# Four edits at the end of a hybrid encoder layer: last stores on ScalarE's queue, a weight sum on GpSimd, low parts regrouped, two row halves finished in PSUM banks

## Chip, core and metric

The kernel runs on one core of a Trainium2 chip. The metric is the device time of one execution in microseconds (us). The engines are called by the profile's names: PE is TensorE (PEld its weight loads), DVE is VectorE, ACT is ScalarE, POOL is GpSimd and SP is SyncE, which in the kernel before issues nearly all DMA transfers.

## The reference

One encoder layer over 1024 tokens and 1024 channels, in float32. What matters here is its end:

```
y_a = attn * silu(z_a);  y_b = h * silu(z_b)
m   = sigmoid(g_a + b0) * (y_a @ w_ba) + sigmoid(g_b + b1) * (y_b @ w_bb)
out = layer_norm(ALPHA * x + m @ w_out, ln_g, ln_b)
```

`y_a` is the attention branch with 512 channels and `y_b` the recurrent one. `x` is the layer's input after an embedding LayerNorm. The last LayerNorm runs over the 1024 channels of each token.

## The kernel before

**Number format.** Every product keeps float32 accuracy with three matmuls on reduced operands: a value is split into a high part (a cast, made on ACT by `high`, line 1317) and a low part (the value minus its high part, made by `lo_of`, line 128, on DVE or POOL), and high times high, low times high and high times low are summed in PSUM (`mm3`, line 134).

**Branch's projection.** The last part of the kernel is a list of numbered slots. In slots 0 to 15 PE multiplies `y_a` by `w_ba`: slot 2j+n is output channel block j (128 channels) and token half n (512 tokens), 12 matmuls each. In the next slot DVE gates the result with g_a (line 1021) and adds the other branch's part (`merge`, line 1331); the sum is a 128x512 block of `m`. The blocks are at once split and combined for the next product.

**Output product.** `m @ w_out` is computed as a 2x2 block product in Strassen-Winograd form: seven products instead of eight. The four blocks of `m` give a11, a12, a22 and the sums s1 to s4; the four blocks of `w_out` give b11, b21, b22 and the sums t1 to t4. Each operand is four tiles of 128x512, c = 0 to 3 (the contraction). `t1(c) = b12 - b11`, `t2(c) = b22 - t1`, `t3(c) = b22 - b12` (written over b12) and `t4(c) = b21 - t2` (written over b21). Slots 16 on walk over PLAN and LAST: a11 times b11 for the four row blocks p = 0 to 3, then a12 with b21, s2 with t2, s1 with t1 for p = 0, 1, s4 with b22 for p = 0, 1, then both for p = 2, 3, then s3 with t3 and a22 with t4. The PSUM bank `banksX[p]` collects a11, s2, s3 and a22, `banksW[p]` a12, s1 and s4. The very last product (a22 with t4, p = 3) is made in two column halves into banks y.

**Evacuation.** After a product, DVE adds the bank to the residual tile `zs[p, r, n]` (128 tokens by 512 channels; r is upper or lower row half of the grid, n the channel half; loaded by `z_load`, line 1413): `begun` (line 1500) or `added` (line 1503), then `seen` (line 1466) takes the row statistics. When both halves of a row are there, `finished(p, r)` runs: `mean_var` (line 1485), `newton` (a square root on ACT at line 1471, a refinement of four small DVE steps, lines 1472 to 1478), the bias on DVE (line 1491), then for each n one ACT pass over z (line 1494), two POOL passes with the gain and the offset (lines 1495 and 1496) and one store from SP (line 1497). This is done for seven of the eight rows. The eighth (p = 3, r = 1) is finished on DVE in quarters (lines 1586 to 1600) with four stores from SP (line 1601).

**What sets the order.** Every engine runs its instructions in the order in which the code is written. `job(slot, f)` puts a function on a slot's list, and the list runs in the order of entry before the slot's product is issued. An instruction that waits holds everything behind it on its engine, and a store that waits holds SP's later transfers. `w_low` (on POOL) reuses, for each new low part, the tile that the `w_low` before it has freed.

Of the kernel before, what the change touches and what calls it, by code (L numbers as in the profile page):

```python
# [25 lines left out]
EPS = 1e-5  # L26
TWICE = 4.0
# [40 lines left out]
def encoder_kernel(ctx, tc, x, gb1, gb, w_qk, w_v, w_s, w_ba, w_bb, w_gate, smalls, bias, w_out, out):  # L68
    nc = tc.nc
    V, A, G, PE, SP = nc.vector, nc.scalar, nc.gpsimd, nc.tensor, nc.sync  # L70

    def pool(name, side="left", **kw):
        return tc.alloc_tile_pool(name=name, bufs=1, side=side, reuse_waits="tile", **kw)
# [131 lines left out]
    halves = [slice(c * HALF, (c + 1) * HALF) for c in range(2)]  # L205
# [83 lines left out]
    def f(t, i):  # L289
        return t[:, :, ti(i)].bitcast(F32)  # L290
# [751 lines left out]
    for slot in range(7 * N_PAIR + 4):  # L1042
        p, k = divmod(slot, 7)
# [184 lines left out]
    for unit in range(-NT, H * NT + PV_LAG):  # L1228
        h, c = divmod(unit, NT)
# [49 lines left out]
        if unit == H * NT:  # L1279
# [3 lines left out]
            wop = pool("wop", "right")  # L1283
            raw = {}
# [18 lines left out]
    def job(slot, f, *args):  # L1303
        jobs.setdefault(slot, []).append(lambda: f(*args))
# [10 lines left out]
    def high(o, c, src, pl, tag, **kw):  # L1315
        t = hi[o, c] = place((o, "h", c), pl, tag, **kw)
        A.copy(t[:], src)

    def low(o, c, src, pl, tag, eng=V):
        t = lo[o, c] = place((o, "l", c), pl, tag)  # L1320
        lo_of(eng, t[:], src, hi[o, c][:])

    def minus(out_, a, b, eng=V):
        eng.tensor_tensor(out_, a, b, ALU.subtract)
# [50 lines left out]
    for slot in range(16):  # L1375
        j, n = divmod(slot, 2)
# [15 lines left out]

    def t3(c):
        t = raw["t3", c] = raw["b12", c]
        minus(t[:], raw["b22", c][:], t[:])

    def t4(c):
        t = raw["t4", c] = raw["b21", c]
# [2 lines left out]
    def w_high(o, c, pl, tag, **kw):  # L1401
        high(o, c, raw[o, c][:], pl, tag, **kw)
# [3 lines left out]
    def w_low(o, c, full, *home):  # L1406
        homes[o, c] = spare.pop()
        spare.append(home)
        low(o, c, full[:], *homes[o, c], G)

    def z_load(p, r, n, pl, tag, **kw):
        z = zs[p, r, n] = pl.tile([P, HALF], F32, tag=tag, name=f"z{p}{r}{n}", **kw)
        SP.dma_start(z[:], h_d[p + 4 * r][:, halves[n]])
# [5 lines left out]
    zs, gbs = {}, {}  # L1419
    for c in range(4):  # L1420
        if c > 1:
            job(c - 2, w_load, "b12", c)
            job(c - 2, w_load, "b11", c)
        job(c + 4, w_load, "b22", c)
        job(c + 6, w_load, "b21", c)
        job(2 * c + 3, t1, c)
        job(2 * c + 4, lambda c: w_high("b11", c, wop, f"b11h{c}"), c)
        job(2 * c + 5, lambda c: w_low("b11", c, raw["b11", c], wop, f"b11{c}"), c)
        job(c + 10, lambda c: w_high("b21", c, *((ap, f"b21h{c}") if c < 3 else (wop, "b21h3"))), c)
        job(16, lambda c: low("b21", c, raw["b21", c][:], yap, f"y1{c}1", G), c)  # L1430
        job(16 + c, lambda c: z_load(c, 0, 0, ev, "z", bufs=5), c)
        job(17, gb_load, c // 2, c % 2)
        job(17, t2, c)
        job(18 + c, t4, c)
        job(17 + c, lambda c: w_high("t2", c, yap, f"y1{c}0"), c)
        job(18 + c, lambda c: w_low("t2", c, raw["t2", c], yap, f"y0{c}1"), c)
        job(18 + c, lambda c: high("s1", c, late["m", c, 1][:], yap, f"y0{c}0"), c)
        job(19 + c, lambda c: w_high("t1", c, ev, *((f"u{c + 1}",) if c < 3 else ("z",)), **({} if c < 3 else dict(bufs=5))), c)
        job(20 + c, lambda c: w_low("s1", c, late["m", c, 1], late["mp"], f"m{c}1"), c)
        job(24 + c, t3, c)  # L1440
        job(21 + c, lambda c: z_load(c, 0, 1, ap, f"a11l{c}"), c)
        job(22 + c, lambda c: w_high("b22", c, wop, f"b11h{c}"), c)
        job(22 + c, lambda c: w_low("t1", c, raw["t1", c], wop, f"t1{c}"), c)
        job(24 + c, lambda c: w_low("b22", c, raw["b22", c], wop, f"b22{c}"), c)
        job(25 + c, lambda c: w_high("t3", c, ap, f"a11h{c}"), c)
        job(25 + c, lambda c: z_load(c, 1, 1, ap, f"a12h{c}"), c)
        job(28 + c, lambda c: w_low("t3", c, raw["t3", c], wop, f"b12{c}"), c)
        job(25 + c, lambda c: high("s3", c, raw["s3", c][:], ap, f"s3h{c}"), c)
        job(27 + c, lambda c: low("s3", c, raw["s3", c][:], *((ap, f"s3l{c - 1}") if c else (wop, "spare3"))), c)
        job(26 + c, lambda c: w_high("t4", c, *homes["b11", c]), c)  # L1450
        job(30 + c, lambda c: w_low("t4", c, raw["t4", c], wop, f"b21{c}"), c)
        job(29 + c, lambda c: z_load(c, 1, 0, ap, f"a12l{c}"), c)

    zp, banksX, banksW, stats = None, {}, {}, {}

    def small(name, n, tag, bufs):
        return zp.tile([P, n], F32, tag=tag, bufs=bufs, name=name)
# [7 lines left out]
            c += n * len(pieces)  # L1465
            V.bn_stats(st[:, 6 * c:6 * c + 6], src[:, part])

    def newton(mv, name, other):

        sd, ve = small(f"sd{name}", 1, "sd", 2), small(f"ve{name}", 3, "ve", 2)  # L1470
        A.activation(sd[:], mv[:, 1:2], AF.Sqrt, bias=eps_z[:])
        V.tensor_scalar(ve[:, 0:1], mv[:, 1:2], EPS * TWICE * TWICE, -0.5, ALU.add, ALU.mult)
        next(other, None)
        V.reciprocal(sd[:], sd[:])
        next(other, None)
        V.tensor_scalar(ve[:, 1:2], sd[:], sd[:], ve[:, 0:1], ALU.mult, ALU.mult)
        next(other, None)
        V.tensor_scalar(sd[:], ve[:, 1:2], 1.5, sd[:], ALU.add, ALU.mult)
        for _ in other:
            pass  # L1480
        return sd, ve

    def mean_var(p, r):
        mv = small(f"mv{p}{r}", 2, "mv", 2)
        V.bn_aggr(mv[:], stats[p, r][:].rearrange("p (c s) -> p c s", s=6))
        return mv

    def finished(p, r):
        mv = mean_var(p, r)
        sd, ve = newton(mv, f"{p}{r}", iter(()))  # L1490
        V.tensor_scalar(ve[:, 2:3], mv[:, 0:1], -1.0, sd[:], ALU.mult, ALU.mult)
        for n in range(2):
            z = zs[p, r, n]
            A.activation(z[:], z[:], AF.Identity, bias=ve[:, 2:3], scale=sd[:])
            G.tensor_tensor(z[:], z[:], gbs[0, n][:], ALU.mult)  # L1495
            G.tensor_tensor(z[:], z[:], gbs[1, n][:], ALU.add)  # L1496
            SP.dma_start(out[p + 4 * r][:, halves[n]], z[:])

    def begun(z, o):
        V.scalar_tensor_tensor(z[:], z[:], ALPHA * TWICE, o[:], ALU.mult, ALU.add)  # L1500
# [46 lines left out]
    for slot in range(16 + len(plan)):  # L1547
        j, n = divmod(slot, 2)
        if slot == 2:
            at0.release()  # L1550
            ap = pool("ap")
            split(0)
        if slot == 3:
            split(1)
        if slot == 16:
            zp = pool("zp")
        if slot < 16 and n == 0 and j > 0:
            b_split(0, j + 1, A)
        for f in jobs.pop(slot, ()):
            f()  # L1560
        if slot < 16:
            if n == 0:
                b_load(0, j + 2)
            g_load(0, j + 1, n, **(dict(tag=f"u{slot % 4}", bufs=1) if slot % 4 else dict(tag="z", bufs=5)))
            o = got[slot] = ring(slot, f"mb{j}{n}")
            run(b_group(0, j, n, ya, o, range(3 if slot < 2 else 4)))
            if 0 < slot < 3:
                run(b_group(0, 0, slot - 1, ya, got[slot - 1], range(3, 4)))
            if 0 < slot < 3:
                merge(slot - 1)  # L1570
            continue
        a, b, p = plan[slot - 16]
        if a == "a11":
            banksX[p] = ring(slot, f"x{p}")
        elif a == "a12":
            banksW[p] = ring(slot, f"w{p}")
        if slot < 16 + len(plan) - 1:
            o = banksX[p] if a in ("a11", "s2", "s3", "a22") else banksW[p]
            o_product(a, b, p, o[:], first=a in ("a11", "a12", "s1"), last=a in ("a12", "s4", "a22"))
    assert not jobs, sorted(jobs)  # L1580

    p, x, w = 3, banksX[3], banksW[3]
    for c, part in enumerate((slice(0, 256), slice(256, HALF))):
        o = ring(c, f"y{c}")
# [4 lines left out]
    mv = mean_var(p, 1)  # L1589

    def scaled():
        for n, part in pieces:
            o = (w, x)[n][:, part]
            V.scalar_tensor_tensor(o, o, mv[:, 0:1], gbs[0, n][:, part], ALU.subtract, ALU.mult)
            yield

    sd, ve = newton(mv, "last", scaled())
    for n, part in pieces:
        z = zs[p, 1, n]
        V.scalar_tensor_tensor(z[:, part], (w, x)[n][:, part], sd[:], gbs[1, n][:, part], ALU.mult, ALU.add)  # L1600
        SP.dma_start(out[p + 4][:, halves[n]][:, part], z[:, part])
# [86 lines left out]
```

## Time and profile before

| what | value |
|---|---|
| median of 3 runs | 673.86 us (673.41 to 674.18) |
| the profiled execution | 674.84 us, of which the span is 673.0 us |
| PE busy | 652.1 us (97%) |
| DVE, ACT, POOL busy | 529.2, 384.6, 403.6 us |
| slots 0 to 15 (branch's projection) | 535.7 to 579.3 us |
| slots 16 on, to PE's last matmul | 579.3 to 657.9 us |
| from PE's last matmul to the end | 15.1 us |

The span is the time between the first and the last recorded event; 1.84 us of the execution's time lie around it. Timeline rows give an instruction's start and duration in us from the span's start, its engine and line, the tiles that it writes and reads, and in brackets how long its engine was idle before it and who ended that. A row with x2 merges two neighbours, and its duration then covers both.

### The profile page before, as it was taken

The numbers are of one execution on the slowest core, as the hardware profiler recorded it, in microseconds if no ns is written. First come the engines' busy times: TensorE is split into PE (matmuls) and PEld (weight loads), VectorE is DVE, ScalarE is ACT, GpSimd is POOL, SyncE is SP. The second block draws the span as 40 slices with busy tenths as digits, with TensorE's granted clock in tenths as the row PEclk, the third lists the DMA queues.
The fourth block names the chain that finished last, engine by engine and source line by source line (L and its number), as shares of the span: only waits on it lengthen the run. The fifth ranks groups of instructions, "written<-read, shape, count | busy, mean of one in ns | idle before, by whom it ended". The sixth has DMA issues, their size and how long they took to land.

```text
span 673.0 us, 9451 instructions
## 1 busy us (share of the span) xinstructions
PE 652.1 (97%) x3129; PEld 543.1 (81%) x3129; DVE 529.2 (79%) x872; ACT 384.6 (57%) x662; POOL 403.6 (60%) x315
## 2 busy tenths in 40 slices
PE   8999999999999999999999999999999999998990
PEld 6888888888888887888788888888888888887880
DVE  6978866986998699879968785377777777996674
ACT  5555433357786676669576634477777645463331
POOL 4898263434676576567647535115264468699996
PEclk9999999999999999999999999999999999999996
DMA  8646616133334123431453547998784496340123
GB/s 325 240 157 220 211 39 216 51 117 118 126 131 137 45 96 125 173 126 47 174 196 105 191 158 261 346 330 306 258 314 165 141 318 215 125 150 7 62 99 121
DMA packets 52337, 113.42 MB, mean 169 GB/s; under 512 B 5488, under 2 KB 10176, under 8 KB 50752
## 3 DMA queue, kind: packets, MB, share of 16 engines
q1 hardware_dynamic: 52256, 112.81, 48.7%
q8 instruction: 25, 0.41, 0.2%
q14 instruction: 24, 0.20, 0.1%
q10 hardware_dynamic: 32, 0.01, 0.0%
HBM read 77.11 MB, written 35.68 MB: 168 GB/s over the span
## 4 chain that ended last, share of the span: by engine, by line
PE 67%; DVE 9%; POOL 9%; issue 4%; ACT 1%; DMA 1%; SPq 0%; POOLq 0%; DVEq 0%; ACTq 0%
PE a L134 28%; PE mb L134 13%; PE s L134 11%; PE acc L1147 4%; PE s L1101 3%; PE x L134 3%; PE pt L1123 3%; POOL z L1495 3%; POOL z L1496 2%; PE g L794 2%; PE w L134 2%; POOL ht_l L128 1%; DVE ws_l L128 1%; DVE wa_l L128 1%; POOL t3l L128 1%
## 5 line engine op out<-in xcount | busy, mean ns | idle before, releaser
L134 PE MATMUL a<-ht_h,ws_h 128*128 128x512 f32 x136 | 53.1, 391 | 0.0
L134 PE MATMUL a<-ht_h,ws_l 128*128 128x512 f32 x136 | 53.0, 389 | 0.0
L134 PE MATMUL a<-b_h,wa_l 128*128 128x512 f32 x136 | 53.0, 389 | 0.0
L134 PE MATMUL a<-b_h,wa_h 128*128 128x512 f32 x136 | 52.9, 389 | 0.0
L134 PE MATMUL a<-ht_l,ws_h 128*128 128x512 f32 x136 | 52.9, 389 | 0.0
L134 PE MATMUL a<-b_l,wa_h 128*128 128x512 f32 x136 | 52.9, 389 | 0.0
L1111 DVE CUSTOM_DVE_ANT_0 sc<-s,bias 128x384 f32<-128x384 f32 (+1 forms) x64 | 33.5, 523 | 21.5 <-PE s L1101 14.1
L1131 ACT CAST pt_h<-pt 128x384 fp32r<-128x384 f32 x64 | 29.0, 453 | 25.3 <-PE pt L1123 17.3
L1116 ACT ACTIVATE p<-sc,summ 128x384 f32<-128x384 f32 (+1 forms) x64 | 37.8, 591 | 5.3 <-DVE summ L1111 5.0
L134 PE MATMUL mb<-ya,wb_h 128*128 128x512 f32 x128 | 39.6, 389 | 0.0
L902 POOL CAST wb_h<-wb 128x512 fp32r<-128x512 f32 x9 | 7.0, 780 | 47.5 <-DMA wb<-in_w_bb_dram 47.5
L128 DVE TENSOR_TENSOR pt_l<-pt,pt_h 128x384 fp32r<-128x384 f32 x64 | 33.3, 520 | 2.1 <-ACT pt_h L1131 1.6
L128 POOL TENSOR_TENSOR ht_l<-t,ht_h 128x512 fp32r<-128x512 f32 x16 | 22.0, 1409 | 19.9 <-ACT ht_h L312 19.9
L326 PE MATMUL v<-wv,b_h 128*128 128x512 f32 x128 | 33.1, 399 | 0.6 <-ACT b_h L279 0.5
L1101 PE MATMUL s<-ks,qs 128*128 128x384 f32 (+1 forms) x128 | 31.4, 326 | 0.0
L134 PEld LDWEIGHTS a<-ht_h,ws_h 128*128 128x128 f32 x136 | 25.5, 188 | 6.0 <-issue 0.4
L1123 PEld LDWEIGHTS pt<-ident,p 128*128 128x128 f32 x176 | 23.1, 140 | 8.5
L134 PEld LDWEIGHTS a<-b_h,wa_h 128*128 128x128 f32 x136 | 25.5, 188 | 5.4
L134 PEld LDWEIGHTS a<-ht_l,ws_h 128*128 128x128 f32 x136 | 25.5, 188 | 5.4
L134 PEld LDWEIGHTS a<-b_l,wa_h 128*128 128x128 f32 x136 | 25.5, 188 | 5.3
L134 PEld LDWEIGHTS a<-b_h,wa_l 128*128 128x128 f32 x136 | 25.5, 188 | 5.3
L134 PEld LDWEIGHTS a<-ht_h,ws_l 128*128 128x128 f32 x136 | 25.5, 188 | 5.2
(541 smaller groups left out, 2270.5 us busy)
## 6 DMA issues: line engine op xcount, KB each, us to landing
ks<-k_d SPq DMA_DIRECT2D x8, 1024.0 KB, 7.4
h_d<-x SPq DMA_DIRECT2D x8, 512.0 KB, 4.4
v_d<-vs SPq DMA_DIRECT2D x8, 512.0 KB, 3.5
q_d<-q SPq DMA_DIRECT2D x8, 512.0 KB, 3.0
ga_d<-ga SPq DMA_DIRECT2D x16, 256.0 KB, 2.2
gb_d<-gb SPq DMA_DIRECT2D x16, 256.0 KB, 2.5
k_d<-k SPq DMA_DIRECT2D x8, 512.0 KB, 3.3
qs<-q_d SPq DMA_DIRECT2D x8, 512.0 KB, 5.5
```

The lines of the kernel that those rows point to most:

```text
L128: eng.tensor_tensor(lo, full, hi.bitcast(F32), ALU.subtract)
L134: PE.matmul(o, a, b, start=first and i == 0, stop=last and i == len(prods) - 1, skip_group_check=not (first and last))
L326: PE.matmul(vos[i][:], a, wv[kind == "w"][k][:], start=vn[i] == 0, stop=vn[i] == 23)
L794: PE.matmul(o[:, n, :], w[:, 2 * d + b, :], us[b][:, n * HALF:(n + 1) * HALF], start=z == 0, stop=z == 1)
L1101: PE.matmul(o[:, :P * len(near(t))], q[:, t * P:(t + 1) * P], k[:, z, keys], start=z == 0, stop=z == 1)
L1111: V.tensor_tensor_reduce(s[:, :w], o[:, :w], heads[h][2][:, b0:b0 + w], -1.0, 3.0e38, ALU.add, ALU.min, accum_out=sums[h][0][:, t:t + 1])
L1116: A.activation(probs[h % 2][t][:], scs.pop((h, t))[:, :w], AF.Exp, bias=sums[h][0][:, t:t + 1], scale=-1.0, accum_out=sums[h][1][:, t:t + 1])
L1123: PE.transpose(tp[:, n * P:(n + 1) * P], probs[h % 2][t][:, z * P:(z + 1) * P], ident[:])
L1131: A.copy(pt[0][:, span(b)], tps[h, b][:, :P * len(near(b))])
L1147: PE.matmul(acc[g][:, d:d + w], vvs[h // 2][:, b, h % 2, :], pt[:, a:a + w], start=b in (1, 6) and z == 0, stop=z == 1 and b == (4, 7)[g])
L1495: G.tensor_tensor(z[:], z[:], gbs[0, n][:], ALU.mult)
L1496: G.tensor_tensor(z[:], z[:], gbs[1, n][:], ALU.add)
```

## The change

Four edits.

1. The four last stores (p = 3, r = 1) are issued on ACT's queue, not on SP's.
2. `t3` is computed on POOL, not on DVE, and in slots 10 to 13, inside the branch's projection, not in slots 24 to 27.
3. POOL's low parts are reordered: the low parts of b22 move from slots 24 to 27 to slots 26 to 29, so that those of t1 come ahead of them; those of t3 and then of t4 all stand in slot 30, ahead of every `finished`. The loads of the z tiles (p, 1, 0) move from slots 29 to 32 to slots 25 to 28.
4. `finished`: the two small steps on the mean and the variance (lines 1472 and 1491 before) go from DVE to three small ACT steps. For the rows (0, 0) and (1, 0), half n = 1, ACT writes its pass into `banksW[p]` in PSUM, and DVE does the gain and the offset there in slots 33 and 34, in place of POOL.

```
     def t3(c):
         t = raw["t3", c] = raw["b12", c]
-        minus(t[:], raw["b22", c][:], t[:])
+        minus(t[:], raw["b22", c][:], t[:], G)
...
-        job(24 + c, t3, c)
+        job(10 + c, t3, c)
...
-        job(24 + c, lambda c: w_low("b22", c, raw["b22", c], wop, f"b22{c}"), c)
+        job(26 + c, lambda c: w_low("b22", c, raw["b22", c], wop, f"b22{c}"), c)
...
-        job(28 + c, lambda c: w_low("t3", c, raw["t3", c], wop, f"b12{c}"), c)
...
-        job(30 + c, lambda c: w_low("t4", c, raw["t4", c], wop, f"b21{c}"), c)
-        job(29 + c, lambda c: z_load(c, 1, 0, ap, f"a12l{c}"), c)
+        job(25 + c, lambda c: z_load(c, 1, 0, ap, f"a12l{c}"), c)
+    for o, home in (("t3", "b12"), ("t4", "b21")):
+        for c in range(4):
+            job(30, lambda o, home, c: w_low(o, c, raw[o, c], wop, f"{home}{c}"), o, home, c)
...
         A.activation(sd[:], mv[:, 1:2], AF.Sqrt, bias=eps_z[:])
-        V.tensor_scalar(ve[:, 0:1], mv[:, 1:2], EPS * TWICE * TWICE, -0.5, ALU.add, ALU.mult)
+        if eng is A:
+            A.activation(ve[:, 0:1], mv[:, 1:2], AF.Identity, bias=eps_h[:], scale=-0.5)
+            A.activation(ve[:, 2:3], mv[:, 0:1], AF.Copy, scale=-1.0)
+        else:
+            V.tensor_scalar(ve[:, 0:1], mv[:, 1:2], EPS * TWICE * TWICE, -0.5, ALU.add, ALU.mult)
...
-        sd, ve = newton(mv, f"{p}{r}", iter(()))
-        V.tensor_scalar(ve[:, 2:3], mv[:, 0:1], -1.0, sd[:], ALU.mult, ALU.mult)
+        sd, ve = newton(mv, f"{p}{r}", iter(()), A)
+        A.activation(ve[:, 1:2], ve[:, 2:3], AF.Copy, scale=sd[:])
         for n in range(2):
             z = zs[p, r, n]
-            A.activation(z[:], z[:], AF.Identity, bias=ve[:, 2:3], scale=sd[:])
+            mine = n == 1 and (p, r) in IN_BANK
+            A.activation((banksW[p] if mine else z)[:], z[:], AF.Identity, bias=ve[:, 1:2], scale=sd[:])
+            if mine:
+                continue
...
+    IN_BANK = ((0, 0), (1, 0))
+
+    def finished_in_bank(p, r):
+        w, z = banksW[p], zs[p, r, 1]
+        V.tensor_tensor(w[:], w[:], gbs[0, 1][:], ALU.mult)
+        V.tensor_tensor(z[:], w[:], gbs[1, 1][:], ALU.add)
+        SP.dma_start(out[p + 4 * r][:, halves[1]], z[:])
+
+    for p, r in IN_BANK:
+        job(33 + p, finished_in_bank, p, r)
...
-        SP.dma_start(out[p + 4][:, halves[n]][:, part], z[:, part])
+        A.dma_start(out[p + 4][:, halves[n]][:, part], z[:, part])
```

**POOL in slots 10 to 16.** Before, POOL's order around the last blocks of the branch's projection is this (wb_l is the low part of a projection weight, a12l that of a block of `m`, b11l and b21l those of `w_out`):

```order
L128 TENSOR_TENSOR a12l_5883<-m_4834,a12h_5849 128x512
L128 TENSOR_TENSOR b11l_5919<-wb_3_5622,b11h_5887 128x512
L128 TENSOR_TENSOR wb_l<-wb_5889,wb_h 128x512
L128 TENSOR_TENSOR a12l_5949<-m_5058,a12h_5908 128x512
L128 TENSOR_TENSOR a12l_6007<-m_5260,a12h_5970 128x512
L128 TENSOR_TENSOR a12l_6060<-m_5468,a12h_6024 128x512
L128 TENSOR_TENSOR b21l_6062<-wb_0_5765,b21h_5885 128x512
```

After, on POOL at the same place (the rows of L1324 are the four t3):

```order
L128 TENSOR_TENSOR a12l_5883<-m_4834,a12h_5849 128x512
L1324 TENSOR_TENSOR wb_0_5572<-wb_0_5708,wb_0_5572 128x512
L1324 TENSOR_TENSOR wb_1_5576<-wb_1_5738,wb_1_5576 128x512
L128 TENSOR_TENSOR b11l_5921<-wb_3_5622,b11h_5888 128x512
L128 TENSOR_TENSOR wb_l<-wb_5890,wb_h 128x512
L128 TENSOR_TENSOR a12l_5951<-m_5058,a12h_5909 128x512
L1324 TENSOR_TENSOR wb_2_5602<-wb_2_5769,wb_2_5602 128x512
L1324 TENSOR_TENSOR wb_3_5620<-wb_3_5801,wb_3_5620 128x512
L128 TENSOR_TENSOR a12l_6011<-m_5260,a12h_5973 128x512
L1577 MEMSET eps_h 128x1
L128 TENSOR_TENSOR a12l_6066<-m_5468,a12h_6028 128x512
L128 TENSOR_TENSOR b21l_6068<-wb_0_5765,b21h_5885 128x512
```

Two t3 stand ahead of the last b11l and the last wb_l, and two ahead of the third a12l.

**POOL's low parts.** Before, from the third low part of t1 on, POOL runs these (z are the passes of `finished`, gb the gain or the offset):

```order
L128 TENSOR_TENSOR b22l_6288<-wb_0_5708,b22h_6237 128x512
L128 TENSOR_TENSOR t1l_6292<-t_5799,t1h_6214 128x512
L128 TENSOR_TENSOR b22l_6316<-wb_1_5738,b22h_6263 128x512
L128 TENSOR_TENSOR t1l_6320<-t_5858,t1h_6245 128x512
L128 TENSOR_TENSOR b22l_6344<-wb_2_5769,b22h_6290 128x512
L128 TENSOR_TENSOR b22l_6370<-wb_3_5801,b22h_6318 128x512
L128 TENSOR_TENSOR t3l_6385<-wb_0_5572,t3h_6309 128x512
L128 TENSOR_TENSOR t3l_6412<-wb_1_5576,t3h_6337 128x512
L128 TENSOR_TENSOR t4l_6431<-wb_0_5765,t4h_6335 128x512
L128 TENSOR_TENSOR t3l_6435<-wb_2_5602,t3h_6363 128x512
L1495 TENSOR_TENSOR z_6064<-z_6064,gb_6094 128x512
```

After, on POOL from the same place on:

```order
L128 TENSOR_TENSOR t1l_6295<-t_5799,t1h_6220 128x512
L128 TENSOR_TENSOR t1l_6322<-t_5858,t1h_6251 128x512
L128 TENSOR_TENSOR b22l_6337<-wb_0_5708,b22h_6243 128x512
L128 TENSOR_TENSOR b22l_6364<-wb_1_5738,b22h_6269 128x512
L128 TENSOR_TENSOR b22l_6391<-wb_2_5769,b22h_6293 128x512
L128 TENSOR_TENSOR b22l_6418<-wb_3_5801,b22h_6320 128x512
L128 TENSOR_TENSOR t3l_6437<-wb_0_5572,t3h_6312 128x512
L128 TENSOR_TENSOR t3l_6439<-wb_1_5576,t3h_6341 128x512
```

Every t1l now stands ahead of every b22l. Behind these rows come the two other t3l, the four t4l and then the first pass over z; before, that pass stood behind the third t3l.

**The end of ACT's queue.** After, ACT's order from the last `finished` (p = 2, r = 1) on is this (rows of DMA are transfers that ACT issues; sd, ve and mv are columns of one number per row; before, no DMA stood here):

```order
L1472 ACTIVATE sd_6755<-mv_6753,eps_z 128x1
L1474 ACTIVATE ve_6756<-mv_6753,eps_h 128x1
L1475 ACTIVATE ve_6756<-mv_6753 128x1
L1496 ACTIVATE ve_6756<-ve_6756,sd_6755 128x1
L1500 ACTIVATE z_6374<-z_6374,ve_6756,sd_6755 128x512
L1500 ACTIVATE z_6370<-z_6370,ve_6756,sd_6755 128x512
L1472 ACTIVATE sdlast<-mv_6802,eps_z 128x1
L1622 DMA out_dram<-z_6401 128x256 x2
L1622 DMA out_dram<-z_6397 128x256 x2
```

The four stores are the last rows of ACT, behind nothing that waits for POOL, and each `finished` has three small rows more on ACT.

More of the change, by code (lines that the diff above doesn't have):

```diff
@@ L1466, in seen, with newton @@
             V.bn_stats(st[:, 6 * c:6 * c + 6], src[:, part])
-    def newton(mv, name, other):
+    def newton(mv, name, other, eng=V):
         sd, ve = small(f"sd{name}", 1, "sd", 2), small(f"ve{name}", 3, "ve", 2)
         A.activation(sd[:], mv[:, 1:2], AF.Sqrt, bias=eps_z[:])
-        V.tensor_scalar(ve[:, 0:1], mv[:, 1:2], EPS * TWICE * TWICE, -0.5, ALU.add, ALU.mult)
+        if eng is A:
[3 more added lines that the diff above has]
+            V.tensor_scalar(ve[:, 0:1], mv[:, 1:2], EPS * TWICE * TWICE, -0.5, ALU.add, ALU.mult)
         next(other, None)
@@ L1556, in encoder_kernel @@
             zp = pool("zp")
+            eps_h = zp.tile([P, 1], F32, name="eps_h")
+            G.memset(eps_h[:], -0.5 * EPS * TWICE * TWICE)
         if slot < 16 and n == 0 and j > 0:
```

## Prediction

> **What bounds the kernel now.** I read the page's chain of work first, then the last rows of each engine, then the waits of SP.
>
> ```profile
> span 673.0 us, 9451 instructions
> PE 67%; DVE 9%; POOL 9%; issue 4%; ACT 1%; DMA 1%; SPq 0%; POOLq 0%; DVEq 0%; ACTq 0%
> ```
>
> PE carries the chain for most of the span, but POOL has 9%, some 60 us. The last rows of each engine show where that share lies:
>
> ```profile
> 657.58 0.28 PE L134 MATMUL y<-t4l,a22h 128*128 128x256 f32 x1
> 660.54 0.29 ACT L1471 ACTIVATE sdlast<-mv,eps_z 128x1 f32<-128x1 f32 x1 [0.58 <-DVE mv L1485]
> 663.36 0.87 DVE L1600 SCALAR_TENSOR_TENSOR z<-x,sdlast,gb 128x256 f32<-128x256 f32 x2
> 664.23 1.26 POOL L1496 TENSOR_TENSOR z<-z,gb 128x512 f32<-128x512 f32 x1
> 665.45 1.26 POOL L1495 TENSOR_TENSOR z<-z,gb 128x512 f32<-128x512 f32 x1
> 666.79 1.26 POOL L1496 TENSOR_TENSOR z<-z,gb 128x512 f32<-128x512 f32 x1
> 668.50 1.86 SPq L1601 DMA_DIRECT2D out_dram<-z  x4
> ```
>
> PE ends at 657.9, ACT at 660.8, DVE at 664.2, POOL at 668.05, and SP issues until 670.4. The four last stores have their data when DVE ends, but the first is issued 4.3 us later, because SP holds them behind a store that waits for POOL:
>
> ```profile
> SPq L1497 <- POOL z L1496: 59.1, 14, 26.4
> L1497 SPq DMA_DIRECT2D out_dram<-z x14: 332/332/338, 629.0 to 668.1; - x14
> L1601 SPq DMA_DIRECT2D out_dram<-z x4: 383/397/408, 668.5 to 670.0; - x4
> DMA to landing us min/median/max: 1.9/2.0/2.2
> ```
>
> The end is thus the last issue (670.0), some 2.1 until it has landed and 0.9 more to the end of the span. Ahead of it POOL is the bound, because it hardly idles in the whole output product:
>
> ```profile
> 582.00:604.00 22.00, 22.00 (x98) 18.14 (x97) 21.07 (x30) 10.78 (x21) 21.53 (x16) 1.00 0.42 135
> 630.00:668.00 38.00, 27.85 (x135) 23.36 (x133) 25.29 (x68) 9.38 (x16) 36.83 (x30) 0.90 0.28 103
> ```
>
> In these two windows (length, then busy time of PE, PEld, DVE, ACT and POOL) POOL is busy 21.5 of 22 and 36.8 of 38 us.
>
> **Stores on ACT's queue.** After its last square root ACT holds nothing that could delay the four stores. This alone takes the end from the last issue of the four (670.0) to POOL's own last store (668.1): **-1.9 us**.
>
> **Two row halves in banks.** They take four of POOL's 28 passes away:
>
> ```profile
> L1495 POOL TENSOR_TENSOR z<-z,gb 128x512 f32<-128x512 f32 x14 | 18.0, 1286 | 1.1 <-ACT z L1494 1.1
> 630.54 0.69 DVE L1500 SCALAR_TENSOR_TENSOR z<-z,w 128x512 f32<-128x512 f32 x1 [1.66 <-PE w L134]
> 633.26 0.69 DVE L1503 TENSOR_TENSOR z<-z,w 128x512 f32<-128x512 f32 x1 [2.03 <-PE w L134]
> ```
>
> A pass starts 1.22 or 1.34 after the one before it (rows above), so four are some 5.2, and POOL would end at 662.8 if its data were there. DVE gets four passes more in slots 33 and 34, at the 0.69 of these rows 2.8 us, and it idles there 1.66 + 2.03 us for PE. I cost them at nothing; without this cover DVE is late by up to 2.8.
>
> The data are not there, however. The last row that POOL finishes gets its ACT pass late:
>
> ```profile
> 657.06 0.29 ACT L1471 ACTIVATE sd<-mv,eps_z 128x1 f32<-128x1 f32 x1 [2.81 <-DVE ve L1472]
> 658.14 0.21 DVE L1491 TENSOR_SCALAR ve<-mv,sd 128x1 f32<-128x1 f32 x1
> 658.45 1.52 ACT L1494 ACTIVATE z<-z,ve,sd 128x512 f32<-128x512 f32 x2 [1.10 <-DVE ve L1491]
> ```
>
> Its first half is ready at 658.45 + 0.76 = 659.2, and four passes of 5.2 to 5.3 us in all end at 664.5. With an empty backlog POOL ends there: 664.5 - 668.05 = **-3.55 us**. From then on POOL follows PE and DVE one for one.
>
> **Small steps on ACT.** Each `finished` loses two DVE steps (one beside the square root, and the 0.21 of L1491 in the path) and gains three on ACT of the kind of the 0.29 row. Two of them run while DVE takes the reciprocal; the third stands where the 0.21 stood. The bounds are -0.2 (all hidden) and +0.7 (all in series); I take **+0.1**, from 0.29 against 0.21.
>
> **Low parts regrouped.** PE stands still once in the output product:
>
> ```profile
> 614.23 0.39 PE L134 MATMUL w<-t1h,s1l 128*128 128x512 f32 x1
> 616.39 0.50 PE L134 MATMUL w<-t1l,s1h 128*128 128x512 f32 x1 [1.77 <-POOL t1l L128]
> 614.74 1.59 POOL L128 TENSOR_TENSOR t1l<-t,t1h 128x512 fp32r<-128x512 f32 x1
> 619.46 0.39 PE L134 MATMUL w<-b22h,s4h 128*128 128x512 f32 x1
> 636.36 1.52 ACT L1494 ACTIVATE z<-z,ve,sd 128x512 f32<-128x512 f32 x2 [1.04 <-DVE ve L1491]
> ```
>
> From 616.39 to 619.46 are 13 matmuls, 0.236 each; at 614.23 the next came after 2.16: 1.9 lost. With t1l ahead of b22l, two POOL operations of about 1.6 leave the queue of the last t1l, which then ends at 613.1, while PE asks at 614.5: the stall goes, **-1.9 us**. Late next is b22l: four at 1.4 from 613.1 end at 618.7, and PE asks for the last 11 matmuls after 619.46 - 1.9, at 620.1. The eight low parts of t3 and t4 then end near 630, and the first two rows' passes near 635. The third row's data (636.36, first half 0.76 later, less what PE gains) come after that, so POOL idles ahead of it and follows PE from there. The z loads come earlier and nothing waits for them: nothing.
>
> **t3 on POOL in the projection.** DVE is spared t3 in a stretch where it idles for PE between them, so the removal gives nothing by itself:
>
> ```profile
> L1324 DVE TENSOR_TENSOR wb<-wb,wb 128x512 f32<-128x512 f32 x4 | 5.6, 1396 | 0.0
> 570.98 1.30 POOL L128 TENSOR_TENSOR wb_l<-wb,wb_h 128x512 fp32r<-128x512 f32 x1 [2.48 <-ACT wb_h L900]
> 574.29 1.29 POOL L128 TENSOR_TENSOR a12l<-m,a12h 128x512 fp32r<-128x512 f32 x1 [0.76 <-ACT m L1339]
> 581.18 1.29 POOL L128 TENSOR_TENSOR a12l<-m,a12h 128x512 fp32r<-128x512 f32 x1 [5.60 <-ACT m L1339]
> ```
>
> POOL has room: it idles 2.48, 0.76 and 5.60 us there, and four t3 at 1.25 to 1.3 take 5.2. The catch is DVE, which works beside POOL there and without a gap:
>
> ```profile
> 567.18 1.32 POOL L128 TENSOR_TENSOR b11l<-wb,b11h 128x512 fp32r<-128x512 f32 x1
> 568.54 0.70 DVE L1324 TENSOR_TENSOR mb<-m,m 128x512 f32<-128x512 f32 x1
> L1324 DVE TENSOR_TENSOR mb<-m,m x4: 699/1220/1575, 568.5 to 588.2; 128x512 f32<-128x512 f32 x4
> L1324 DVE TENSOR_TENSOR mb<-m,mb x4: 685/685/685, 571.1 to 591.0; 128x512 f32<-128x512 f32 x4
> ```
>
> The subtraction of two SBUF tiles (m, m) takes 0.70 when POOL is idle, as at 568.54, when b11l has just ended, and 1.2 to 1.6 the other three times; with one input in PSUM (mb) it is always 0.685. After, a t3 runs at 568.5, so this one joins the slow three. DVE has no gap to 600 to recover in; the last a12l waits for it through ACT, and all of POOL behind it is late by as much. POOL's next deadline is tight:
>
> ```profile
> 602.10 1.29 POOL L128 TENSOR_TENSOR t2l<-t,t2h 128x512 fp32r<-128x512 f32 x1
> 603.55 0.39 PE L134 MATMUL x<-t2l,s2h 128*128 128x512 f32 x1
> ```
>
> The last t2l ends at 603.4 and PE takes it at 603.55, so nearly all of DVE's delay becomes a new stall. Its bounds are 0 (DVE gets in between two t3) and 1.8 (0.9 at this subtraction and as much again at the next, which is slow already). I take **+0.9**, the slowest of the four rows (1.575 - 0.7).
>
> On this the Trainium skill, page "SBUF — State Buffer", section "Who interferes with whom", says that a DVE instruction with two SBUF inputs contends with a GpSimd instruction that reads SBUF, and that whoever issues first has the shared ports for its whole length. It speaks against this edit; the 0.70 and the 1.22 agree with it in kind.
>
> **Sum.** Against the profiled execution (span 673.0, time 674.84): stores -1.9, POOL's end -3.55, ACT steps +0.1, old stall -1.9, new stall +0.9, together -6.35: a span of 666.65. On the other queue DVE's last piece comes at 664.2 - 1.0 = 663.2, its store is issued by 663.6, and POOL's at 663.65: they end together. The profiled execution lies 0.98 above the median of 673.86, which the change has no reason to alter; the same 6.35 off the median is **667.5 us**.
>
> **The rivals.**
> - *No new stall.* DVE gets in ahead of the t3. For it: 568.54 is only 0.1 behind the place where a t3 would start (567.18 + 1.25). Against: three of four such subtractions are slow. 667.5 - 0.9 = 666.6. Chance 0.22.
> - *A wait for the whole t3.* DVE asks 0.1 after the second t3 has started and gets nothing until it ends: +1.15, and the next subtraction, which then falls on another t3, takes 1.575 and not 1.22: +0.35. The stall is 1.5 in place of 0.9: 668.1. This is what the page named above would have. For it: the row with 1.575. Against: two of three slow ones lose only 0.5. Chance 0.20.
> - *More delay.* On top of it the ACT steps are in series, or the stores of two queues share bandwidth, or DVE's bank passes miss their cover: +0.6 to +2.8, 668.4 to 670.3. Each is small alone. Chance 0.12.
> - *The gain does not appear.* POOL stays the bound, since its first pass comes at 630 and not at 626.3 (after the third t3l). Then 3.7 + 668.05 - 5.2 = 666.55, and with the stores -3.4: 670.5. Against: those 24 passes end at 662 if never idle. Chance 0.03.
> - *Slower.* The two t3 ahead of wb_l hold it, and PE takes that weight in slot 14:
>
> ```profile
> 535.89 43.57 PE mb L134 x192
> L1289 SPq DMA_DIRECT2D wb<-in_w_out_dram x16: 327/400/1481, 533.6 to 556.2; - x16
> DMA to landing us min/median/max: 3.7/5.5/6.7
> ```
>
> 16 slots in 43.6 us make slot 14 start at 574.0; wb_l ends at 572.3 now and near 573 after. From 574.0 on each us of wb_l is one of PE. To eat 6.35 it has to end past 580, as when a t3 waits for its b22; the last of those loads was issued by 556.2 and landed by 563. Chance 0.02.
>
> **How the numbers follow.** The forecast (667.5, itself 667.0 to 668.0) has 0.41. The range goes from the first rival with the ACT steps hidden and half of them gained (666.1) to the middle of *more delay* (669.4). A measurement here can tell some 0.2%, 1.35 us, from no change; faster means below 672.5. Only the last rival passes that, and part of the one ahead of it comes near: faster 0.96, same 0.02, slower 0.02.
>
> **What would show it.** No wait of PE for t1l; a wait for t2l of about 0.9 near 603.6; the subtraction at 568.5 at 1.2 or more; POOL's last pass ending near 663.6, with an idle gap ahead of each row's first pass; ACT issuing four stores between 661.5 and 663.6. It is wrong if PE waits in the projection, if POOL's passes run to the end without gaps, or if SP or ACT issues later than 665.

## The result and the profile after

| | before | after |
|---|---|---|
| median (lowest to highest, 7 runs each) | 674.18 us (673.41 to 674.52) | 669.56 us (668.78 to 672.83) |
| ratio, 95% interval | | 0.9942 [0.9924, 0.9960] |
| profiled execution, its span | 674.84 us, 673.0 us | 670.15 us, 668.4 us |

The kernel became faster by 3.9 us by the ratio (4.6 between the two medians) where 6.35 were forecast, and 669.56 lies just above the range of 666.1 to 669.4. Slot 0 does not begin at the same time in all executions (533.9 to 535.9 us over the runs below), though nothing ahead of it was changed. So profiles are compared by their **tail**: the span less the start of slot 0's first matmul. Before it is 673.0 - 535.73 = 137.27 us, after 668.4 - 535.52 = 132.88: **-4.39 us**.

The first lines of the page after, and the waits of PE from 535 to 670 us (us in total, times, longest):

```profile
span 668.4 us, 9464 instructions
PE 81%; DVE 8%; POOL 3%; DMA 3%; issue 2%; SPq 1%; ACT 1%; POOLq 0%; DVEq 0%; ACTq 0%
```

```profile
PE x L134 <- POOL t2l L128: 1.8, 1, 1.8
PE mb L134 <- POOL wb_l L128: 0.3, 1, 0.3
```

POOL's share of the chain fell from 9% to 3%, as edit 4 intends. The wait for t1l is gone, but two waits for POOL stand in its place. PE's timeline, before and then after, says what they cost (the first row of each is slot 0's first matmul; x<-b11h is the output product's first):

```profile
535.73 0.39 PE L134 MATMUL mb<-ya,wb_h 128*128 128x512 f32 x1
...
579.30 0.39 PE L134 MATMUL x<-b11h,a11h 128*128 128x512 f32 x1
```

```profile
535.52 0.40 PE L134 MATMUL mb<-ya,wb_h 128*128 128x512 f32 x1
...
573.61 0.61 PE L134 MATMUL mb<-ya,wb_h 128*128 128x512 f32 x2
574.54 0.50 PE L134 MATMUL mb<-ya,wb_l 128*128 128x512 f32 x1 [0.31 <-POOL wb_l L128]
...
579.91 0.39 PE L134 MATMUL x<-b11h,a11h 128*128 128x512 f32 x1
...
603.95 0.39 PE L134 MATMUL x<-t2h,s2l 128*128 128x512 f32 x1
606.11 0.50 PE L134 MATMUL x<-t2l,s2h 128*128 128x512 f32 x1 [1.77 <-POOL t2l L128]
...
620.07 0.39 PE L134 MATMUL w<-b22h,s4h 128*128 128x512 f32 x1
```

Slots 0 to 15 took 43.57 us before (579.30 - 535.73) and take 44.39 now (579.91 - 535.52): 0.82 is lost. Of this 0.47 are at the wait for wb_l in slot 14 (0.93 from 573.61 to 574.54, where 0.46 is usual) and 0.16 come behind it. The other 0.19 lie ahead of slot 14 (573.61 is 38.09 behind the start, before it was 37.90) and belong to no wait. From 603.95 to 606.11 are 2.16 where 0.23 is usual: 1.93 lost. From 579.91 to 620.07 are 40.16, just what it was before (579.30 to 619.46): in this stretch the stall at t2l has eaten the whole gain of the one at t1l. Together PE loses **0.82 + 1.93 = 2.75 us** in the places of the new waits, the 0.19 included.

Where the waits come from is seen on DVE, ACT and POOL, in their timelines of after:

```profile
568.53 2.94 DVE L1324 TENSOR_TENSOR mb<-m,m 128x512 f32<-128x512 f32 x1
...
577.14 1.67 DVE L1324 TENSOR_TENSOR mb<-m,m 128x512 f32<-128x512 f32 x1
```

```profile
571.50 0.59 ACT L1317 CAST s2h<-mb 128x512 fp32r<-128x512 f32 x1 [3.08 <-DVE mb L1324]
...
572.50 0.62 ACT L900 CAST wb_h<-wb 128x512 fp32r<-128x512 f32 x1
```

```profile
567.08 2.58 POOL L1324 TENSOR_TENSOR wb<-wb,wb 128x512 f32<-128x512 f32 x2
569.58 1.33 POOL L128 TENSOR_TENSOR b11l<-wb,b11h 128x512 fp32r<-128x512 f32 x1
573.20 1.28 POOL L128 TENSOR_TENSOR wb_l<-wb,wb_h 128x512 fp32r<-128x512 f32 x1 [2.29 <-ACT wb_h L900]
...
575.70 2.54 POOL L1324 TENSOR_TENSOR wb<-wb,wb 128x512 f32<-128x512 f32 x2
578.21 1.74 POOL L128 TENSOR_TENSOR a12l<-m,a12h 128x512 fp32r<-128x512 f32 x1
...
583.85 1.29 POOL L128 TENSOR_TENSOR a12l<-m,a12h 128x512 fp32r<-128x512 f32 x1 [3.86 <-ACT m L1339]
...
604.79 1.27 POOL L128 TENSOR_TENSOR t2l<-t,t2h 128x512 fp32r<-128x512 f32 x1
```

The subtraction at 568.53 took 2.94 us, not 0.70. It started 0.2 into the second t3 and ended at 571.47, that is 0.56 after b11l (570.91): it stood behind the rest of one t3 *and* the whole of b11l. The next one (577.14) took 1.67, not 1.22: it came 0.2 into a t3 too, but got in when that one had ended, and the a12l behind (578.21) took 1.74, not 1.29. ACT needs the first result for s2h (571.50) before it comes to wb_h (572.50), so POOL's wb_l came at 573.20, not 570.98 (+2.22), and ended at 574.48, past the 574.0 at which PE asks. The last a12l came at 583.85, not 581.18 (+2.67), and the last t2l at 604.79, not 602.10 (+2.69).

The end of the kernel, by ACT's timeline, POOL's timeline and the rows of out_dram, all of after:

```profile
657.53 0.28 ACT L1474 ACTIVATE ve<-mv,eps_h 128x1 f32<-128x1 f32 x1
657.71 0.19 ACT L1475 ACTIVATE ve<-mv 128x1 f32<-128x1 f32 x1
658.54 0.29 ACT L1496 ACTIVATE ve<-ve,sd 128x1 f32<-128x1 f32 x1 [0.64 <-DVE sd L1483]
658.87 1.52 ACT L1500 ACTIVATE z<-z,ve,sd 128x512 f32<-128x512 f32 x2
```

```profile
654.32 1.29 POOL L1503 TENSOR_TENSOR z<-z,gb 128x512 f32<-128x512 f32 x1 [0.16 <-ACT z L1500]
...
659.76 1.27 POOL L1503 TENSOR_TENSOR z<-z,gb 128x512 f32<-128x512 f32 x1 [0.17 <-ACT z L1500]
...
663.67 1.26 POOL L1504 TENSOR_TENSOR z<-z,gb 128x512 f32<-128x512 f32 x1
```

```profile
L1505 SPq DMA_DIRECT2D out_dram<-z x12: 332/332/338, 634.7 to 665.0; - x12
L1622 ACTq DMA_DIRECT2D out_dram<-z x4: 370/414/482, 663.2 to 664.7; - x4
```

POOL idles for ACT ahead of a row's first pass, so it follows its data; it ends at 664.93 (668.05 before). ACT issues its four stores from 663.2 to 664.7 and SP its last at 665.0: the two queues end together. From there to the end of the span are 3.4 us, where before 3.0 lay behind the last issue (670.0).

### The profile page after: what moved, and what is told of

The parts are those of the page before. It is cut to its first block, busy times and chain, and to the rows that moved or that the text cites. A ratio compares the mean times of both kernels' runs of the same rounds, so it can differ in the third digit from the quotient of the medians.

```text
span 668.4 us, 9464 instructions
## 1 busy us (share of the span) xinstructions
PE 652.8 (98%) x3129; PEld 543.4 (81%) x3129; DVE 526.7 (79%) x858; ACT 388.1 (58%) x683; POOL 402.6 (60%) x316
## 4 chain that ended last, share of the span: by engine, by line
PE 81%; DVE 8%; POOL 3%; DMA 3%; issue 2%; SPq 1%; ACT 1%; POOLq 0%; DVEq 0%; ACTq 0%
PE a L134 32%; PE s L134 11%; PE mb L134 9%; PE v L326 6%; PE x L134 4%; PE acc L1147 4%; PE q L134 3%; PE w L134 3%; PE s L1101 3%; PE pt L1123 3%; PE g L794 2%; DMA wqk_s<-in_w_qk_dram 2%; DVE ws_l L128 1%; PE tp L270 1%; DVE wa_l L128 1%
```

## The experiments

**The theory**: the whole miss is edit 2. A t3 on POOL beside DVE's subtraction of two SBUF tiles costs that subtraction 2.7 us in two steps, PE pays it at wb_l and t2l, and the other three edits give what the sum said. **Its rivals**: the loss lies in another edit (the regrouped low parts, stores of two queues side by side, ACT's steps), the edits do not add, or t3 costs POOL's time wherever it stands. Each run was compared with runs of the kernel before on the same chip (medians 674.15 to 674.57).

| kernel | median (lowest to highest, runs) | ratio | tail against before's 137.27 |
|---|---|---|---|
| after, t3 back on DVE | 666.71 (666.6 to 666.94, 4) | 0.9885 [0.9870, 0.9900] | -7.42 |
| after, t3 in slot 15 | 666.93 (665.85 to 667.27, 4) | 0.9884 [0.9871, 0.9898] | -7.10 |
| before, with edit 2 | 675.67 (674.79 to 676.56, 11) | 1.0020 [1.0011, 1.0029] | +2.17 |
| before, with edit 1 | 671.40 (671.09 to 672.33, 5) | 0.9956 [0.9943, 0.9968] | -1.74 |
| before, with edit 3 | 672.95 (672.29 to 674.77, 10) | 0.9980 [0.9971, 0.9989] | -0.87 |
| before, with edit 4 | 670.53 (670.09 to 672.27, 5) | 0.9944 [0.9932, 0.9956] | -3.63 |
| before, with edits 1 and 4 | 669.71 (668.78 to 670.48, 5) | 0.9928 [0.9916, 0.9940] | -5.14 |
| after, all t3 in slot 10 | 671.42 (668.19 to 672.16, 6) | 0.9944 [0.9928, 0.9961] | -2.72 |
| after, all t3 in slot 13 | 667.45 (666.78 to 667.64, 4) | 0.9898 [0.9882, 0.9915] | -6.91 |
| after, a second profile | 670.04 (one run) | | -4.90 |
| after, subtraction from one SBUF input | 666.76 (666.42 to 668.08, 4) | 0.9892 [0.9873, 0.9912] | -7.40 |
| both: that, and t3 in slot 15 | 666.45 (665.84 to 666.9, 4) | 0.9884 [0.9869, 0.9899] | -7.41 |

### t3 back on DVE

After, with edit 2 undone:

```
-        minus(t[:], raw["b22", c][:], t[:], G)
+        minus(t[:], raw["b22", c][:], t[:])
-        job(10 + c, t3, c)
+        job(24 + c, t3, c)
```

> The changed kernel with the t3 edit alone undone: t3 is again on DVE in slots 24 to 27, all else as changed. Theory A (the t3 on POOL blocked DVE's subtraction of two SBUF tiles: 2.94 us at 568.5 and 1.67 at 577.1 where it took 0.70 and 1.22 before, POOL's chain came 2.67 late and PE waited 0.3 for wb_l and 1.8 for t2l): the subtraction takes 0.70 again, PE waits for neither, PE's end moves some 2.5 us forward and POOL's with it: about 2.5 us less than the changed kernel, 667.0 us. Theory B (the three new steps on ACT or the regrouped low parts cost it): no difference to the changed kernel, 669.5 us, and the wait for t2l stays.

666.71 us. PE's waits list neither wb_l nor t2l; the first subtraction in DVE's timeline, and PE's rows (the same stretches as above):

```profile
567.73 0.70 DVE L1324 TENSOR_TENSOR mb<-m,m 128x512 f32<-128x512 f32 x1
```

```profile
534.95 0.39 PE L134 MATMUL mb<-ya,wb_h 128*128 128x512 f32 x1
...
578.49 0.39 PE L134 MATMUL x<-b11h,a11h 128*128 128x512 f32 x1
...
616.59 0.39 PE L134 MATMUL w<-b22h,s4h 128*128 128x512 f32 x1
```

Slots 0 to 15 take 43.54 us (44.39 after) and the next stretch 38.10 (40.16): both new waits are gone, and t1l's has not come back. The tail is shorter by 7.42; the prediction's sum without its new stall is 6.35 + 0.9 = 7.25. So the other three edits give together what the sum said, and edit 2 costs the changed kernel 2.9 us between the medians (669.56 and 666.71).

### t3 on POOL, but in slot 15

```
-        job(10 + c, t3, c)
+        job(15, t3, c)
```

> The changed kernel with all four t3 on POOL in slot 15, behind the third a12l, where POOL idled 5.6 us before and DVE has no subtraction of two SBUF tiles until 581.8. Theory A (only the collision with that subtraction costs, not POOL's work): DVE's first two subtractions take 0.70 and about 1.2, PE waits for no t2l or at most 0.3, about 667.0 us. Theory B (POOL has no room for four more operations ahead of the weight low parts, wherever they stand): PE waits 1.5 or more for t2l again, 669.5 us.

666.93 us, no wait of PE. DVE's first two subtractions, and POOL's four t3 with the last a12l behind them:

```profile
566.95 0.70 DVE L1324 TENSOR_TENSOR mb<-m,m 128x512 f32<-128x512 f32 x1
...
573.32 1.22 DVE L1324 TENSOR_TENSOR mb<-m,m 128x512 f32<-128x512 f32 x1
```

```profile
573.95 5.50 POOL L1324 TENSOR_TENSOR wb<-wb,wb 128x512 f32<-128x512 f32 x4
...
579.59 1.29 POOL L128 TENSOR_TENSOR a12l<-m,a12h 128x512 fp32r<-128x512 f32 x1
```

The same four t3 on the same engine cost nothing measurable where POOL idles for the last a12l and DVE's subtraction is over. It is the place, not the engine.

### Each edit alone

Before with edit 2 alone:

```
-        minus(t[:], raw["b22", c][:], t[:])
+        minus(t[:], raw["b22", c][:], t[:], G)
-        job(24 + c, t3, c)
+        job(10 + c, t3, c)
```

> The kernel before with only the t3 edit (on POOL in slots 10 to 13). Theory A: the subtraction at 568.5 takes 2.9, PE waits for wb_l and t2l (2.5 us in all) and for about 1 us at t1l; POOL, which is the bound of the tail here, starts its output-product chain 2.7 late and gets some 1.3 back since DVE's t3 no longer compete with it: 1.0 to 2.0 us slower than before, 675.4 us. Theory B (the delay of PE is what counts one for one): 2.5 us slower or more, 676.7 us. Theory C (t3 on POOL is free): 674.0 us.

675.67 us, slower by 1.4: the edit is a loss in itself. Its DVE and PE rows show the same two marks as after:

```profile
567.54 2.83 DVE L1324 TENSOR_TENSOR mb<-m,m 128x512 f32<-128x512 f32 x1
```

```profile
573.45 0.50 PE L134 MATMUL mb<-ya,wb_l 128*128 128x512 f32 x1 [0.20 <-POOL wb_l L128]
```

PE waits for t2l too (1.7 us), but not at t1l, where about 1 us was expected. In this profile PE's granted clock was 0.72 from 604 to 608 and 0.90 from 608 to 614, so it came to t1l later; no other profile here shows this, and what the other ten runs had of it is not known. The total met its forecast, one of its terms did not.

Before with edit 1 alone:

```
-        SP.dma_start(out[p + 4][:, halves[n]][:, part], z[:, part])
+        A.dma_start(out[p + 4][:, halves[n]][:, part], z[:, part])
```

> The kernel before with only the four last stores moved to ACT's queue. Theory A (they only queued behind POOL's last store): the last issue comes at 668.1 and not at 670.0, 1.9 us less: 672.2 us. Theory B (the last 256 KB transfer then ends the span and takes about 0.4 longer from its issue to the end, as in the changed kernel's trace, 3.4 against 3.0): 1.5 us less, 672.6 us.

671.40 us; -1.74 in the tail against -1.9. By medians it is -2.85, more than the tail shows; in the two profiles another 0.76 lie ahead of slot 0 (534.97 against 535.73), where nothing was changed. The rows of out_dram show the hold gone: ACT's stores are issued 3.6 us ahead of SP's last one.

```profile
L1497 SPq DMA_DIRECT2D out_dram<-z x14: 332/332/338, 628.3 to 667.4; - x14
L1601 ACTq DMA_DIRECT2D out_dram<-z x4: 368/401/413, 662.4 to 663.8; - x4
```

Before with edit 3 alone (the low parts and the z loads, as in the diff of the change):

```
-        job(24 + c, lambda c: w_low("b22", c, raw["b22", c], wop, f"b22{c}"), c)
+        job(26 + c, lambda c: w_low("b22", c, raw["b22", c], wop, f"b22{c}"), c)
-        job(28 + c, lambda c: w_low("t3", c, raw["t3", c], wop, f"b12{c}"), c)
...
-        job(30 + c, lambda c: w_low("t4", c, raw["t4", c], wop, f"b21{c}"), c)
-        job(29 + c, lambda c: z_load(c, 1, 0, ap, f"a12l{c}"), c)
+        job(25 + c, lambda c: z_load(c, 1, 0, ap, f"a12l{c}"), c)
+    for o, home in (("t3", "b12"), ("t4", "b21")):
+        for c in range(4):
+            job(30, lambda o, home, c: w_low(o, c, raw[o, c], wop, f"{home}{c}"), o, home, c)
```

> The kernel before with only the low parts regrouped (and the z loads moved with them). Theory A (PE's stall at t1l goes, but POOL is the bound of the tail and has the same operations to do): from slot 0 to the end 0 to 1.1 us less than before (1.1 is POOL's one idle gap ahead of its first pass), about 673.5 us. Theory B (PE's stall is on the path to the end): 1.9 us less, 672.3 us.

672.95 us: PE's 1.9 us are gained and only 0.87 arrive in the tail (1.6 by medians), because POOL's passes, still 28, then run without a gap to the end and bound it:

```profile
663.63 1.26 POOL L1496 TENSOR_TENSOR z<-z,gb 128x512 f32<-128x512 f32 x1
664.97 1.26 POOL L1497 TENSOR_TENSOR z<-z,gb 128x512 f32<-128x512 f32 x1
```

Before with edit 4 alone (`finished`, `newton` and `finished_in_bank` as in the diff of the change):

```
-            A.activation(z[:], z[:], AF.Identity, bias=ve[:, 2:3], scale=sd[:])
+            mine = n == 1 and (p, r) in IN_BANK
+            A.activation((banksW[p] if mine else z)[:], z[:], AF.Identity, bias=ve[:, 1:2], scale=sd[:])
...
+    for p, r in IN_BANK:
+        job(33 + p, finished_in_bank, p, r)
```

> The kernel before with only the finished rows changed: two row halves in banks on DVE, three small steps on ACT. Theory A (the backlog of POOL is worked off, and the last row's data bind): POOL's last pass ends 3.5 us earlier, 670.6 us. Theory B (POOL stays the bound): 5.2 us earlier, 668.9 us. Theory C (DVE or ACT become late by the added steps): less than 2 us gained.

670.53 us, -3.63 in the tail against -3.55 + 0.1. POOL has four passes less and ends bound by ACT's pass, as costed:

```profile
658.28 1.27 POOL L1502 TENSOR_TENSOR z<-z,gb 128x512 f32<-128x512 f32 x1 [0.17 <-ACT z L1499]
```

Before with edits 1 and 4 (the two diffs above together):

> The kernel before with the stores on ACT's queue and the finished rows in banks, but neither t3 nor the low parts moved. Theory A (the terms add up): 1.8 + 3.5 = 5.3 us less than before, 668.8 us, and PE still waits 1.8 us for t1l. The difference to the first run above (all but t3, 666.7) is then what the regrouping is worth once POOL has no backlog: 1.9 us. Theory B (the regrouping is worth nothing): 666.9 us.

669.71 us, -5.14 in the tail where the two alone give 1.74 + 3.63 = 5.37: they add. With edit 3 on top this is *after with t3 back on DVE* (-7.42), so edit 3, worth 0.87 alone, is worth 2.3 once POOL no longer bounds the end.

### How far the wait goes

After, all four t3 in slot 10, back to back ahead of b11l:

```
-        job(10 + c, t3, c)
+        job(10, t3, c)
```

> The changed kernel with all four t3 in slot 10, back to back ahead of b11l. Theory A (DVE gets the shared access only when POOL pauses, as when it lost to t3 and then to b11l behind it): the subtraction at 568.5 waits for three t3 and b11l, 5 to 6 us, and the kernel is 1.5 to 3 us slower than the changed one, 671 to 672.5 us. Theory B (DVE waits for the running operation and at times for one more): the subtraction takes 1.2 to 3 us, 667.5 to 669.6 us.

671.42 us. DVE's subtraction, POOL's row beside it, and PE in slot 14:

```profile
568.66 5.36 DVE L1324 TENSOR_TENSOR mb<-m,m 128x512 f32<-128x512 f32 x1
```

```profile
567.18 5.03 POOL L1324 TENSOR_TENSOR wb<-wb,wb 128x512 f32<-128x512 f32 x4
572.18 1.28 POOL L128 TENSOR_TENSOR b11l<-wb,b11h 128x512 fp32r<-128x512 f32 x1
```

```profile
575.73 0.50 PE L134 MATMUL mb<-ya,wb_h 128*128 128x512 f32 x1 [1.59 <-ACT wb_h L900]
...
577.08 0.50 PE L134 MATMUL mb<-ya,wb_l 128*128 128x512 f32 x1 [0.85 <-POOL wb_l L128]
```

One DVE instruction of 0.70 us took 5.36: it came 0.2 into the second of five POOL instructions and ended 0.56 after the fifth (573.46), when POOL idled. The wait grew with the row of POOL work behind it. One of the six runs took 668.19, the five others 671.3 to 672.2; whether that one escaped the wait is not shown.

After, all four t3 in slot 13, where the second subtraction meets them:

```
-        job(10 + c, t3, c)
+        job(13, t3, c)
```

> The changed kernel with all four t3 in slot 13, back to back between the second and the third a12l, so that DVE's second subtraction of two SBUF tiles (near 575) meets a run of t3, and the first one meets b11l's end as before the change. Theory A (a run of POOL operations without a pause keeps DVE out until the run ends): the second subtraction takes 4 to 5 us, PE waits 2 us or more for t2l, 669.5 to 671 us. Theory B (DVE gets in behind the operation that is running, and the losses at 568.5 belong to that place): it takes 1.2 to 1.7, 667 us.

667.45 us. DVE's second subtraction and POOL's row beside it:

```profile
574.33 1.67 DVE L1324 TENSOR_TENSOR mb<-m,m 128x512 f32<-128x512 f32 x1
```

```profile
572.90 5.50 POOL L1324 TENSOR_TENSOR wb<-wb,wb 128x512 f32<-128x512 f32 x4
```

My theory that an unbroken row of t3 keeps DVE out until it ends **fell** here: DVE came again 0.2 into the second t3 and got in behind that one. PE still waits 0.2 us for t2l. The repeated loss was seen only at 568.5, at the first of the four subtractions.

The changed kernel itself, profiled once more:

> The changed kernel itself, a second profiled execution. Theory A (which of DVE and POOL goes first is the same each time): the subtraction at 568.5 takes 2.9 us again and the time is 669 to 671 us. Theory B (it differs from execution to execution, and this is why the changed kernel's seven times spread from 668.8 to 672.8): another duration, 0.7 to 1.8 or above 4, with a time to match.

```profile
L1324 POOL TENSOR_TENSOR wb<-wb,wb x4: 1287/1308/1312, 567.0 to 576.9; 128x512 f32<-128x512 f32 x4
L1324 DVE TENSOR_TENSOR mb<-m,m x4: 1227/1610/2749, 568.6 to 590.8; 128x512 f32<-128x512 f32 x4
```

670.04 us; in its rows of L1324 (least, median and most ns) the longest subtraction takes 2.75 us, again the first one, behind a t3 and b11l. The loss repeats, PE's price a little lower: slots 0 to 15 take 44.01 us, 0.44 more than before, and 1.89 are lost at t2l (603.88 to 606.00), 2.33 in all.

### The subtraction with one SBUF input

After, with t3 where the change put it. With m0 and m1 for the two tiles of `m`, `second` makes s2 = (m1 + o) - m0 from two SBUF tiles. Since s3 = m0 - m1 is there already, it is written as o - s3, with o in PSUM, for the same value:

```
-        minus(o[:], late["m", c, 1][:], late["m", c, 0][:])
+        minus(o[:], o[:], raw["s3", c][:])
```

> The changed kernel, t3 where the change put it, but DVE's subtraction takes the block from its PSUM bank and subtracts s3 (already computed on POOL) from it, instead of subtracting two SBUF tiles: same value, one SBUF input. Theory A (it is the second SBUF input that POOL's operations block): all four subtractions take 0.69, PE waits neither for wb_l nor for t2l, POOL's chain starts at least as early as before the change: 666.7 us or up to 1 us less, as the other three subtractions get faster too. Theory B (POOL's four more operations ahead of the low parts are what delays it, whatever DVE does): PE's waits stay, 669.5 us.

666.76 us, no wait of PE. The rows of L1324:

```profile
L1324 POOL TENSOR_TENSOR wb<-wb,wb x4: 1299/1302/1307, 566.5 to 574.3; 128x512 f32<-128x512 f32 x4
L1324 DVE TENSOR_TENSOR mb<-mb,s x4: 692/692/693, 568.1 to 586.3; 128x512 f32<-128x512 f32 x4
```

All four take 0.69 us beside the same t3. The tail (-7.40) is that with t3 on DVE (-7.42): nothing of edit 2's cost is left. The whole cost hung on the subtraction's second SBUF input.

Both together, this and t3 in slot 15:

> The same one-SBUF-input subtraction with t3 in slot 15. Theory A (no collision is left in either place): the same time as the run beside it within 0.5 us, 666 to 666.7 us. Theory B (t3 in slot 15 and the collision are worth something of their own each): 1 us less than the run beside it.

666.45 us, the lowest median here, though within 0.5 us of the three others without the collision. Once it is gone, the place of t3 makes no difference that these runs can tell.

## Why the prediction was wrong

The direction held, and so did the mechanism of edits 1, 3 and 4. **The step that failed is the new stall** of edit 2, taken at +0.9 with bounds of 0 and 1.8: it let DVE wait for one POOL instruction and lead to one wait of PE. The runs put 2.75 us in its place (2.33 in the second profile): DVE waited for a t3 and for b11l behind it, and PE paid twice, at wb_l and at t2l.

| term | forecast | measured | where |
|---|---|---|---|
| stores on ACT's queue | -1.9 | -1.5 | last issue is POOL's store, 665.0; 0.4 more behind it |
| POOL's end, with ACT's steps | -3.45 | -3.6 | edit 4 alone |
| old stall at t1l | -1.9 | -1.9 | 1.93 of t2l balanced in 40.16 against 40.16 |
| new stall | +0.9 | +2.75 | 0.82 in slots 0 to 15 (0.19 of it ahead of slot 14), 1.93 at t2l |
| sum | -6.35 | -4.25 (the tail: -4.39) | |

- **The bound was too low because its rows were.** It took the slowest subtraction of before (1.575) as the worst case. In those rows DVE stood behind one POOL instruction. The change put three in a row there (two t3, then b11l), and DVE stood behind parts of two: +2.24, and +0.45 at the next. One t3 alone costs 0.97, as at 577.14 (1.67 - 0.70), so 0.9 was a fair size for one; b11l added the other 1.27. A bound from rows of another arrangement was no bound.
- **The slow rows of before were misread.** The prediction held against a wait for a whole POOL instruction that two of the three lose only 0.5. But they came 0.63 us into an a12l and ended 0.56 after it; this is the second subtraction in DVE's timeline of before, beside the a12l at 574.29 that the prediction shows:

```profile
574.92 1.22 DVE L1324 TENSOR_TENSOR mb<-m,m 128x512 f32<-128x512 f32 x1
```

- **The rival that named the mechanism was mis-sized too.** *A wait for the whole t3* (668.1) priced one POOL instruction at this place. The Trainium skill, page "SBUF — State Buffer", section "Who interferes with whom", lets the loser wait for the whole length of the other's instruction; 1.67 us at 577.14 agrees (it ended 0.57 after the t3), 2.94 and 5.36 go beyond one instruction.
- **The slower rival came true in small, by another cause.** It named wb_l, slot 14 and the point 574.0, and wb_l ended at 574.48. But it let the two t3 hold wb_l and put its end near 573. POOL was through with them and with b11l at 570.91 and idled 2.29 us for wb_h: ACT holds wb_h behind s2h, which waits for the subtraction. By the prediction's own list, PE waiting in the projection was a sign against it.
- **Right**: the hold of the stores; the last row's data and not 5.2 us of passes as POOL's new bound; the bank passes hidden in DVE; and that ACT's steps cost next to nothing. In the row before the last, from the start of DVE's `mean_var` to ACT's pass, it is 1.79 us now (651.64 to 653.43) and was 1.70 (651.03 to 652.73), the 0.1 of the forecast. In the last row, the one that counts, it is 1.79 (657.08 to 658.87) and was 1.97 (656.48 to 658.45): there it became 0.18 shorter.
- **Missed besides**: 0.4 us between the last issue and the end; *more delay* had named the two queues.
- **Slips in its sums**: in *more delay*, 667.5 + 0.6 is 668.1, not 668.4, which would put the upper end of the range at 669.2; and 666.6 with all of ACT's steps hidden is 666.3, not 666.1. The result lies above the range either way.

What stays open is why DVE's first subtraction (c = 0) lost to the POOL instructions that followed, once in each of three profiles and three times in a row with all t3 in slot 10, while the three later ones got in behind the running one in every trace. They came about as early into it: 0.19 to 0.36 us where DVE lost, 0.18 to 0.20 where it met a t3 and got in. Operation, engines and tile sizes were the same. A cause for the difference was not found.

## What to carry to other kernels

Before work is moved to GpSimd, look at what VectorE does at that time: an instruction there with two SBUF inputs can wait for several GpSimd instructions in turn, so the price can be the length of the unbroken row and not one overlap; here one place paid it each time that it was profiled, and the others did not. Give such an instruction a PSUM input, or put the moved work where GpSimd idles for something that comes after it; either gave back all of the 2.9 us here. And follow a late instruction through every engine that queues behind it: here the same late subtraction reached PE by two ways, some 30 us apart.

## What the runs showed of the hardware

- A VectorE subtraction of 128x512 with two SBUF inputs took 0.70 us alone and 1.22, 1.67, 2.94 or 5.36 beside GpSimd; with one of its inputs in PSUM it took 0.69 in all four cases.
- GpSimd's own rows show only half of the collisions. Those that kept VectorE waiting for longer took their usual 1.27 to 1.34 us (the t3 and b11l beside the 2.94, 2.75 and 5.36); where VectorE got in, the GpSimd instruction behind took 1.74 and not 1.29 (a12l at 578.21).
- From the last store's issue to the end of the span were 3.0 to 3.1 us where the last store followed others on its own queue (before, edit 3, edit 4 alone) or came 3.6 us behind ACT's (edit 1 alone), and 3.3 to 3.4 where ACT's and SP's last ones came within 0.3 us (after, edits 1 and 4, t3 back on DVE). That the two queues' stores slow each other is a reading of this and was not tried by itself; the size of the last store is not it, since edit 1 alone ends with the same 128x512 store.
